# A two-layer hybrid decoder trunk: the mixer's products in joined 512-column form, its branches one after another, and its value products in pairs

## The chip, the core and the metric

The kernel runs on one core of one Trainium2 chip. A core has five engines with an instruction queue each: TensorE (PE; its weight loads are listed as PEld), VectorE (DVE), ScalarE (ACT), GpSimd (POOL) and SyncE (SP), which here issues the loads of weights. The metric is the device time of one execution in microseconds (us).

## The reference

Two layers of three residual blocks each on a sequence of 256 tokens of width 1024; all is float32.

```python
for l in range(DEPTH):
    x = x + 0.5 * swiglu(rmsnorm(x, norm_ffn1[l]), w_ffn1_in[l], w_ffn1_out[l])
    h = rmsnorm(x, norm_mix[l])
    x = x + hybrid_mixer(h, ...)
    x = x + 0.5 * swiglu(rmsnorm(x, norm_ffn2[l]), w_ffn2_in[l], w_ffn2_out[l])
# hybrid_mixer
a_qkv, b_q, b_kv, c_q, c_k, c_v, c_glow, c_r, gate_pre = jnp.split(h @ w_in, splits, axis=-1)
y_a = dilated_mixer(a_q, a_k, a_qkv[:, :, 2])          # 3 groups of 8 heads, merged by softmax denominators
o_b, _ = band_attention(...); y_b = o_b.reshape(...)   # 8 query heads on 2 key heads, with sinks
o_c = gla_chunked(...)                                 # gated linear attention, a recurrence over chunks
y_c = (rmsnorm(o_c, c_out_norm) * jax.nn.silu(c_r)).reshape(...)
gates = jax.nn.sigmoid(gate_pre.reshape(bn, s, N_BRANCH, D_MODEL))
merged = (gates[:, :, 0] * (y_a @ w_branch[0])
          + gates[:, :, 1] * (y_b @ w_branch[1])
          + gates[:, :, 2] * (y_c @ w_branch[2]))
return merged @ w_out
```

## The kernel before

Every matrix product is made in three parts, since TensorE takes the operands in a rounded float32 form. A weight w is split into hi, the rounded w, and lo = w - hi; the activation x likewise into two parts. The sum hi*x_hi + hi*x_lo + lo*x_hi stands for w*x. Weights come from memory as "raw" tiles of 128x1024 (four buffers); for each *unit* of 8 weight blocks of 128x128, ACT casts raw to hi (L191) and DVE subtracts to get lo (L192). There are five buffers each of hi and lo, and the split runs four units ahead of the product, so the split of unit u+5 can begin only when the product of unit u no longer needs its hi (ACT) and its lo (DVE).

A product with 256 tokens as columns has two forms:

- `mm3` (L330): three matmuls of 256 columns for each block, with three weight loads (L331, L332, L333), all into one 256-column half of a PSUM bank.
- `mmw` (L335): the two parts of x lie side by side in one tile, so that hi is loaded once for 512 columns (L341), and lo once for 256 columns (L343). The bank then holds two halves, which `joined` (L345) adds: ACT copies the upper half to a tile "low" (L347), DVE adds (L348).

Before the change the feed-forward blocks use `mmw`, and the mixer's feature-major products use `mm3`: the keys and queries of the linear attention (ck, cq), the 24 gate products, the three branch projections (12 units) and the output product w_out (8 units), 48 units in each layer. Token-major products (`tok_proj`, L541 to L543) are not touched.

PSUM has eight banks: four ("mm") rotate through these products, four ("at") through attention, transposes and the norm. A bank is free when the last reader of its former tile is done.

The attention ("att") and the linear recurrence ("gla") are generators; `fill` advances them by a rate after each product, so that their steps stand between the products on PE. After the gates all generators are run to the end, then the branches are taken per pair of output tiles (`mp`), all three branches in turn, and the merged tile is split once more into hi and lo (mh, ml), the input of w_out.

The program is written in this order, but a scheduler of the framework, which simulates it, decides at build time in which order each engine's instructions stand. Each engine then works through its list in that order and waits, where it must, with all that stands behind.

Other lines named below: the sum of squares of the norm is made on PE by L315, taken up by DVE in L316; POOL makes the reciprocal root r from it (L256), and PE spreads r over partitions (L324). L560 and L565 are the rotary embedding's products on DVE, which read a product's bank, L606 the scaling of the rotated key, L579 a transpose on PE, L571 and L597 small steps around POOL's root. L686 is the product of attention weights and values (AV), L761 a POOL copy that spreads a merge weight over a head.

## Time and profile before

| | before |
|---|---|
| median of 3 runs | 1452.05 us (1452.04 to 1452.5) |
| profiled execution, its own time | 1451.91 us |
| span of the trace | 1449.8 us |
| PE / PEld busy | 1439.2 us (99%) / 1268.1 us (87%) |
| DVE / ACT / POOL busy | 1053.7 us (73%) / 834.3 us (58%) / 137.9 us (10%) |
| data from memory | 246.31 MB, mean 170 GB/s |
| granted clock of PE | 0.999 of 2.4 GHz |

The span is what the trace covers; the execution's own time has 2.1 us more around it. The chain of waits goes back from the last instruction and tells which engine the time was spent on. A duration is that of one instruction's record. Records of instructions that follow each other on an engine overlap a little, so the pace of a series is read from starts, not from durations.

### The profile page before, as it was taken

The page shows a single profiled execution, that of the slowest core. Times are in us where ns is not written, and L with a number is a line of the kernel's source. Part 1 is how long each engine was busy: PE and PEld are TensorE (multiplying, and loading weights), DVE is VectorE, ACT ScalarE, POOL GpSimd, SP SyncE. Part 2 cuts the span into 40 slices and gives each one's busy share as a digit, 9 for nine tenths or more (in the row PEclk, how much of TensorE's full clock was granted, in tenths as well). Part 3 has the DMA queues.
Part 4 walks back from the last instruction along what each step waited for, and adds up shares of the span by engine and source line. Part 5 has one row for each costly group of instructions (what it writes and reads, how often), then busy time and mean ns, then how long its engine had stood idle before and what let it go on. Part 6 is the DMA issues. An engine that isn't in the chain of part 4 may idle for free.

```text
span 1449.8 us, 23394 instructions
## 1 busy us (share of the span) xinstructions
PE 1439.2 (99%) x9114; PEld 1268.1 (87%) x9114; DVE 1053.7 (73%) x1923; ACT 834.3 (58%) x1432; POOL 137.9 (10%) x124
## 2 busy tenths in 40 slices
PE   8999999999999999999999999999999999999998
PEld 6888898888899998888888888988878999988887
DVE  6887667888677687776677766688876767776753
ACT  6665456556747456565466555466477464566542
POOL 2030012223111000000000000131210200000000
PEclk9999999999999999999999999999999999999999
DMA  9665564443552565655665655643444426565651
GB/s 297 213 197 172 170 213 146 146 145 117 156 164 74 176 217 179 199 178 178 196 195 183 194 170 168 208 153 128 147 144 146 146 74 218 175 204 176 198 183 54
DMA packets 214702, 246.31 MB, mean 170 GB/s; under 512 B 6524, under 2 KB 183376, under 8 KB 214592
## 3 DMA queue, kind: packets, MB, share of 16 engines
q1 hardware_dynamic: 214016, 243.48, 52.2%
q0 software_dynamic: 544, 1.33, 0.4%
q8 instruction: 71, 1.16, 0.3%
q14 instruction: 39, 0.32, 0.1%
q10 hardware_dynamic: 32, 0.01, 0.0%
HBM read 243.76 MB, written 1.05 MB: 169 GB/s over the span
## 4 chain that ended last, share of the span: by engine, by line
PE 95%; DVE 2%; ACT 1%; POOL 1%; DMA 1%; issue 0%; SPq 0%; DVEq 0%
PE p L341 30%; PE p L343 16%; PE p L333 6%; PE p L331 6%; PE p L332 6%; PE p L541 6%; PE p L543 5%; PE p L542 5%; PE p L650 2%; PE p L686 2%; PE p L579 1%; PE p L485 1%; PE p L486 1%; PE p L487 1%; PE p L695 1%; PE p L874 1%
## 5 line engine op out<-in xcount | busy, mean ns | idle before, releaser
L191 ACT CAST hi<-raw 128x1024 fp32r<-128x1024 f32 (+3 forms) x468 | 484.2, 1037 | 509.1 <-PE p L341 270.9
L192 DVE TENSOR_TENSOR lo<-raw,hi 128x1024 fp32r<-128x1024 f32 (+3 forms) x468 | 564.8, 1209 | 255.1 <-ACT hi L191 249.2
L341 PE MATMUL p<-a,hi 128*128 128x512 f32 x1936 | 491.3, 394 | 1.5 <-ACT hi L191 1.2
L341 PEld LDWEIGHTS p<-a,hi 128*128 128x128 f32 x1936 | 348.5, 189 | 65.4 <-ACT hi L191 2.5
L343 PEld LDWEIGHTS p<-a,lo 128*128 128x128 f32 x1936 | 265.4, 190 | 19.3
L343 PE MATMUL p<-a,lo 128*128 128x256 f32 x1936 | 272.1, 282 | 0.0
L333 PE MATMUL p<-a,lo 128*128 128x256 f32 x768 | 219.0, 285 | 0.0
L331 PE MATMUL p<-a,hi 128*128 128x256 f32 x768 | 218.1, 285 | 0.0
L332 PE MATMUL p<-a,hi 128*128 128x256 f32 x768 | 218.0, 284 | 0.0
L256 POOL TENSOR_TENSOR s<-s,neghalf 128x8 f32<-128x8 f32 (+2 forms) x42 | 90.8, 2161 | 974.7 <-DVE s L316 656.1
L541 PE MATMUL p<-hi,a 128*128 128x512 f32 (+1 forms) x416 | 163.5, 393 | 0.0
L542 PE MATMUL p<-lo,a 128*128 128x512 f32 (+1 forms) x416 | 162.1, 390 | 0.0
L543 PE MATMUL p<-hi,a 128*128 128x512 f32 (+1 forms) x416 | 161.3, 389 | 0.0
L333 PEld LDWEIGHTS p<-a,lo 128*128 128x128 f32 x768 | 147.0, 191 | 1.4 <-issue 1.4
L332 PEld LDWEIGHTS p<-a,hi 128*128 128x128 f32 x768 | 147.0, 191 | 0.7 <-issue 0.3
L331 PEld LDWEIGHTS p<-a,hi 128*128 128x128 f32 x768 | 146.6, 191 | 1.1 <-issue 0.7
L541 PEld LDWEIGHTS p<-hi,a 128*128 128x128 f32 x416 | 79.3, 191 | 16.0 <-issue 0.7
L542 PEld LDWEIGHTS p<-lo,a 128*128 128x128 f32 x416 | 79.3, 191 | 14.6 <-issue 0.3
L543 PEld LDWEIGHTS p<-hi,a 128*128 128x128 f32 x416 | 79.0, 191 | 15.0 <-issue 0.3
L347 ACT COPY low<-p 128x256 f32<-128x256 f32 x200 | 74.5, 372 | 0.7 <-PE p L343 0.5
L348 DVE TENSOR_TENSOR w<-p,low 128x256 f32<-128x256 f32 x176 | 73.4, 418 | 0.0
L671 ACT ACTIVATE w<-w,st,s 128x128 f32<-128x128 f32 (+1 forms) x96 | 47.8, 504 | 11.7 <-DVE st L665 11.7
(224 smaller groups left out, 1294.7 us busy)
## 6 DMA issues: line engine op xcount, KB each, us to landing
raw<-in_w_ffn_in_dram SPq DMA_DIRECT2D x87, 1024.0 KB, 5.1
raw<-in_w_in_dram SPq DMA_DIRECT2D x76, 1024.0 KB, 5.1
raw<-in_w_ffn_out_dram SPq DMA_DIRECT2D x34, 1024.0 KB, 5.3
raw<-in_w_branch_dram SPq DMA_DIRECT2D x24, 512.0 KB, 3.4
raw<-in_w_ffn_out_dram SPq DMA_DIRECT2D x12, 768.0 KB, 4.5
raw<-in_w_out_dram SPq DMA_DIRECT2D x8, 1024.0 KB, 5.7
raw<-in_w_in_dram SPq DMA_DIRECT2D x4, 512.0 KB, 3.8
a<-in_x_dram SPq DMA_DIRECT2D x4, 256.0 KB, 4.6
```

The source lines that it names most:

```text
L191: nc.scalar.copy(hi[:, k:k + cut], r[:, k:k + cut])
L192: nc.vector.tensor_sub(lo[:, k:k + cut], r[:, k:k + cut], f(hi[:, k:k + cut]))
L256: nc.gpsimd.tensor_tensor(dst, src, neghalf[:, 0:n], op=OP.pow)
L331: nc.tensor.matmul(ps, wh, xh, start=first, stop=False)
L332: nc.tensor.matmul(ps, wh, xl, start=False, stop=False)
L333: nc.tensor.matmul(ps, wl, xh, start=False, stop=last)
L341: nc.tensor.matmul(ps, wh[:, k, :], xhl[k], start=first and k == 0, stop=False)
L343: nc.tensor.matmul(ps[:, 0:T], wl[:, k, :], xhl[k][:, 0:T], start=False, stop=last and k == nk - 1)
L347: nc.scalar.copy(low, ps[:, T:2 * T])
L541: nc.tensor.matmul(o, xh, wh[:, k - k0, :], start=(k == 0), stop=False)
L542: nc.tensor.matmul(o, xh, wl[:, k - k0, :], start=False, stop=False)
L543: nc.tensor.matmul(o, xl, wh[:, k - k0, :], start=False, stop=(k == KD - 1))
```

## The change

The mixer's products all use `mmw` with `joined`. Each 256-column product now takes a bank of its own (before, two shared one), and the gate's and key's scaling (L985, L990 before) reads the joined tile instead of the bank. The branches are taken in the order 2, 0, 1, each with all its four mp before the next; before a branch, only the generator that it needs is run to the end (`waits`), so that the other generators' steps may stand between its products; the weights of the branches are loaded in that order. Branch outputs are kept as tiles with both parts side by side (`y_parts`: twice as many instructions of half the size). The merged tile is split per 256 columns when the last branch has been added (L1056, L1057). w_out is taken in pairs of output tiles, the first pair in two steps of 6 and 2 blocks. In the attention, two AV groups are issued together. In the changed kernel the lines of the helpers are: split cast L192 and subtraction L193, `mmw` L337 and L339, `joined` L343 and L344, norm L316, L317 and L325, transpose L575.

```diff
+ORDER = (2, 0, 1)
...
-                for mp in range(KD // 2):
-                    for i in range(3):
+                for i in ORDER:
+                    for mp in range(KD // 2):
...
-
-    def mm3(ps, wh, wl, xh, xl, first, last):
-        nc.tensor.matmul(ps, wh, xh, start=first, stop=False)
-        nc.tensor.matmul(ps, wh, xl, start=False, stop=False)
-        nc.tensor.matmul(ps, wl, xh, start=False, stop=last)
...
-        def feat_proj(o):
-            wh, wl = chunk()
-            for k in range(KD):
-                mm3(o, wh[:, k, :], wl[:, k, :], n.h[k], n.l[k], k == 0, k == KD - 1)
+        def feat_proj():
+            ps = bank("mm")
+            mmw(ps, chunk(), n.hl, True, True)
+            return ps
...
-                    if pts:
-                        av(*pts.pop())
                     pts.append((i0, pt))
                     yield
-                av(*pts.pop())
+                    if len(pts) == 2:
+                        for a in pts:
+                            av(*a)
+                        pts.clear()
                 yield from done(t, o) if sink is None else done(t, o, nb, den)
 
         yT = [[None] * 4 for _ in range(3)]
+        merged = []
 
         def new_y(i):
             yT[i] = [big(F32R) for _ in range(4)]
 
         def y_parts(i, e, cols, src):
 
-            hv, lv = v3(yT[i][e], 2)[:, :, cols], v3(yT[i][2 + e], 2)[:, :, cols]
-            nc.scalar.copy(hv, src)
-            nc.vector.tensor_sub(lv, src, f(hv))
+            for u in range(2):
+                hv, lv = yT[i][2 * e + u][:, 0:T][:, cols], yT[i][2 * e + u][:, T:2 * T][:, cols]
+                nc.scalar.copy(hv, src[:, u])
+                nc.vector.tensor_sub(lv, src[:, u], f(hv))
...
+            merged.append(True)
...
-        ps = bank("mm")
-        feat_proj(ps[:, 0:T])
+        pk = [feat_proj()]
...
-        feat_proj(ps[:, T:2 * T])
+        pk.append(feat_proj())
         ck = big()
-        nc.vector.tensor_mul(v3(ck, 2), v3(ps, 2), rb2)
-        ps = bank("mm")
         for j in range(2):
-            feat_proj(ps[:, j * T:(j + 1) * T])
+            joined(ck[:, j * T:(j + 1) * T], pk[j])
+        nc.vector.tensor_mul(v3(ck, 2), v3(ck, 2), rb2)
         cq = big()
-        nc.vector.scalar_tensor_tensor(v3(cq, 2), v3(ps, 2), HD ** -0.5, rb2, op0=OP.mult, op1=OP.mult)
+        for j in range(2):
+            joined(cq[:, j * T:(j + 1) * T], feat_proj())
+        nc.vector.scalar_tensor_tensor(v3(cq, 2), v3(cq, 2), HD ** -0.5, rb2, op0=OP.mult, op1=OP.mult)
...
-            ps = bank("mm")
+            g = big()
             for j in range(2):
-                feat_proj(ps[:, j * T:(j + 1) * T])
+                ps = feat_proj()
                 fill()
-            g = big()
-            nc.vector.tensor_mul(v3(g, 2), v3(ps, 2), rb2)
+                joined(g[:, j * T:(j + 1) * T], ps)
+            nc.vector.tensor_mul(v3(g, 2), v3(g, 2), rb2)
             nc.scalar.activation(g, g, AF.Tanh, scale=0.5)
             gates.append(g)
-        while streams:
-            for name in list(streams):
-                step(name)
-        mh, ml = [], []
-        for mp in range(KD // 2):
-            acc = gates[mp]
-            for i in range(3):
-                wh, wl = chunk()
-                ps = bank("mm")
+        def waits(i):
+            return ("att" in streams and not merged) if i == 0 else ("att" if i == 1 else "gla") in streams
+
+        mhl = []
+        for i in ORDER:
+            while waits(i):
+                for name in list(streams):
+                    step(name)
+            for mp in range(KD // 2):
+                acc, g = gates[ORDER[0] * 4 + mp], gates[i * 4 + mp]
+                w = chunk()
+                o = wrk()
                 for j in range(2):
-                    for k in range(4):
-                        sl = slice((k % 2) * T, (k % 2) * T + T)
-                        mm3(ps[:, j * T:(j + 1) * T], wh[:, k, j * P:(j + 1) * P], wl[:, k, j * P:(j + 1) * P],
-                            yT[i][k // 2][:, sl], yT[i][2 + k // 2][:, sl], k == 0, k == 3)
-                g = gates[i * 4 + mp]
-                nc.vector.scalar_tensor_tensor(g, g, 1.0, ps, op0=OP.add, op1=OP.mult)
-                if i:
-                    nc.vector.tensor_add(acc, acc, g)
-            h, lo = big(F32R), big(F32R)
-            nc.scalar.copy(h, acc)
-            nc.vector.tensor_sub(lo, acc, f(h))
-            mh.append(h)
-            ml.append(lo)
-        for m in range(KD):
-            wh, wl = chunk()
-            ps = bank("mm")
-            for k in range(KD):
-                sl = slice((k % 2) * T, (k % 2) * T + T)
-                mm3(ps[:, 0:T], wh[:, k, :], wl[:, k, :], mh[k // 2][:, sl], ml[k // 2][:, sl], k == 0, k == KD - 1)
-            nc.vector.scalar_tensor_tensor(xT[m], ps[:, 0:T], 0.5, xT[m], op0=OP.mult, op1=OP.add)
-            nxt(m)
+                    ps = bank("mm")
+                    mmw(ps, [a[:, :, j * P:(j + 1) * P] for a in w], yT[i], True, True)
+                    joined(o[:, j * T:(j + 1) * T], ps)
+                    fill()
+                nc.vector.scalar_tensor_tensor(g, g, 1.0, o, op0=OP.add, op1=OP.mult)
+                if i == ORDER[0]:
+                    continue
+                nc.vector.tensor_add(acc, acc, g)
+                if i == ORDER[2]:
+                    for j in range(2):
+                        hl = big(F32R)
+                        a = acc[:, j * T:(j + 1) * T]
+                        nc.scalar.copy(hl[:, 0:T], a)
+                        nc.vector.tensor_sub(hl[:, T:2 * T], a, f(hl[:, 0:T]))
+                        mhl.append(hl)
+        for m0 in range(0, KD, 2):
+            ws = [chunk(), chunk()]
+            pss = [bank("mm"), bank("mm")]
+            for ks in (slice(0, KD - 2), slice(KD - 2, KD)) if m0 == 0 else (slice(0, KD),):
+                for j in range(2):
+                    mmw(pss[j], [w[:, ks, :] for w in ws[j]], mhl[ks], ks.start == 0, ks.stop == KD)
+            for j in range(2):
+                m = m0 + j
+                tmp = sm.tile([P, T], F32, tag="res", bufs=2, name=nm("res"))
+                joined(tmp, pss[j])
+                nc.vector.scalar_tensor_tensor(xT[m], tmp, 0.5, xT[m], op0=OP.mult, op1=OP.add)
+                nxt(m)
```

**Start of the mixer, DVE.** After the last step of the norm's sum (acc190), L316 (now L317) takes the sum from PE's bank p240; lo74 to lo76 are splits of weights for units 74 to 76. Before:

```order
L300 TENSOR_TENSOR acc190_1666<-acc190_1666,sq220_2101 128x256
L316 TENSOR_SCALAR s241_2202<-p240_2201 128x4
L192 TENSOR_TENSOR lo74_2214<-raw39_2002,hi74_2213 128x1024
L192 TENSOR_TENSOR lo75_2295<-raw39_2002,hi75_2294 128x1024
L972 SCALAR_TENSOR_TENSOR s229_2132<-s242_2208 128x4
L973 TENSOR_SCALAR s230_2133<-s242_2208 128x4
```

After:

```order
L301 TENSOR_TENSOR acc190_1666<-acc190_1666,sq220_2101 128x256
L193 TENSOR_TENSOR lo74_2214<-raw39_2002,hi74_2213 128x1024
L317 TENSOR_SCALAR s241_2202<-p240_2201 128x4
L193 TENSOR_TENSOR lo75_2288<-raw39_2002,hi75_2287 128x1024
L193 TENSOR_TENSOR lo76_2320<-raw40_2024,hi76_2319 128x1024
L971 SCALAR_TENSOR_TENSOR s229_2132<-s242_2208 128x4
```

The first reading of the norm's sum now stands behind the split lo74, and one more split (lo76) ahead of the small steps that use r.

**Start of the mixer, PE.** p240 is the norm's bank, s242 its root r. Between the sum's matmuls (L315, now L316) and this place stand 31 instructions of products before, and 15 after (14 of 256 columns, L339, and one of 512, L337). Before:

```order
L331 MATMUL p266_2324<-a188_1661,hi72_2145 128x256
L332 MATMUL p266_2324<-a188_1661,hi72_2145 128x256
L333 MATMUL p266_2324<-a188_1661,lo72_2146 128x256
L331 MATMUL p266_2324<-a195_1794,hi72_2145 128x256
L324 MATMUL p240_2201<-cst_70,s242_2208 128x128 x2
L332 MATMUL p266_2324<-a195_1794,hi72_2145 128x256
```

After:

```order
L339 MATMUL p265_2286<-a215_2086,lo71_2065 128x256
L339 MATMUL p265_2286<-a219_2098,lo71_2065 128x256
L325 MATMUL p240_2201<-cst_70,s242_2208 128x128 x2
L337 MATMUL p270_2316<-a184_1650,hi72_2145 128x512
L337 MATMUL p270_2316<-a188_1661,hi72_2145 128x512
```

What stands behind r's spreading is now the first product into bank p270, the bank of the token product p238, which L556 and L561 (L560 and L565 before) still have to read; before, p266 had been begun ahead of it, and no bank of p238 or p239 was needed for ck and cq.

**Start of w_out, DVE.** lo161 and lo162 are splits for the fourth and fifth unit of w_out; p779 and p781 are the two halves of the last branch unit; a683, a693 are merged tiles and a762 the first of the eight split tiles for w_out. Before:

```order
L192 TENSOR_TENSOR lo161_5634<-raw88_5431,hi161_5633 128x1024
L1046 SCALAR_TENSOR_TENSOR a674_5261<-a674_5261,p692_5637 128x512
L1048 TENSOR_TENSOR a611_4560<-a611_4560,a674_5261 128x512
L192 TENSOR_TENSOR lo162_5671<-raw89_5468,hi162_5670 128x1024
L1051 TENSOR_TENSOR a694_5665<-a611_4560,a693_5664 128x512
L1060 SCALAR_TENSOR_TENSOR xT0_106<-p695_5674,xT0_106 128x256
```

After:

```order
L193 TENSOR_TENSOR lo161_5534<-raw88_5319,hi161_5533 128x1024
L344 TENSOR_TENSOR w771_5500<-p774_5513,low775_5522 128x256
L1051 TENSOR_TENSOR a683_4873<-a683_4873,a630_4517 128x512
L1048 SCALAR_TENSOR_TENSOR a648_4634<-a648_4634,w764_5461 128x512
L344 TENSOR_TENSOR w778_5537<-p779_5538,low780_5547 128x256
L1048 SCALAR_TENSOR_TENSOR a659_4716<-a659_4716,w771_5500 128x512
L193 TENSOR_TENSOR lo162_5573<-raw89_5352,hi162_5572 128x1024
L344 TENSOR_TENSOR w778_5537<-p781_5550,low782_5559 128x256
L1057 TENSOR_TENSOR a762_5451<-a683_4873,a762_5451 128x256
L1051 TENSOR_TENSOR a693_4941<-a693_4941,a648_4634 128x512
```

The join of the last half (L344 of p781) and the first part for w_out (L1057, a762) now stand behind lo162; the four merged tiles come ready one after another behind it.

**Start of w_out, PE.** hi157 and lo157 are the last branch unit's weights, hi158 to hi161 those of w_out. Before:

```order
L332 MATMUL p692_5637<-a571_4301,hi157_5502 128x256
L333 MATMUL p692_5637<-a569_4299,lo157_5503 128x256
L331 MATMUL p695_5674<-a678_5362,hi158_5535 128x256
L332 MATMUL p695_5674<-a679_5363,hi158_5535 128x256
L333 MATMUL p695_5674<-a678_5362,lo158_5536 128x256
```

After:

```order
L339 MATMUL p781_5550<-a680_4858,lo157_5388 128x256
L339 MATMUL p781_5550<-a681_4859,lo157_5388 128x256
L337 MATMUL p785_5580<-a762_5451,hi158_5420 128x512
L337 MATMUL p786_5581<-a762_5451,hi159_5457 128x512
L337 MATMUL p796_5646<-a762_5451,hi160_5496 128x512
L337 MATMUL p797_5647<-a762_5451,hi161_5533 128x512
L337 MATMUL p785_5580<-a763_5454,hi158_5420 128x512
```

Before, the first product of w_out takes a678 and a679, made from the first merged tile, which was complete nine units earlier; now it takes a762, and four products take each tile in turn.

## Rows read from the trace of the kernel before

**Rows 1.** Busy time and share of the span of each engine, and the chain of waits by engine.

```profile
PE 1439.2 (99%) x9114; PEld 1268.1 (87%) x9114; DVE 1053.7 (73%) x1923; ACT 834.3 (58%) x1432; POOL 137.9 (10%) x124
PE 95%; DVE 2%; ACT 1%; POOL 1%; DMA 1%; issue 0%; SPq 0%; DVEq 0%
```

**Rows 2.** What PE waited for between 25 and 1440 us, all of it: total us, times, longest.

```profile
PE p L579 <- DVE a L599: 0.6, 2, 0.3
```

**Rows 3.** The chain in a feed-forward stretch (`mmw`): start us, length us, what.

```profile
601.59 1.84 PE p L341 x8
603.43 0.95 PE p L343 x8
...
612.76 1.84 PE p L341 x8
```

**Rows 4.** The chain in the branch stage (`mm3`), the first and the last of 34 pieces without a gap: start us, length us, what.

```profile
517.98 0.12 PE p L332
...
521.94 0.12 PE p L332
```

**Rows 5.** Groups of instructions by line and shape: busy us, mean ns of one.

```profile
L331 PE MATMUL p<-a,hi 128*128 128x256 f32 x768 | 218.1, 285 | 0.0
L192 DVE TENSOR_TENSOR lo<-raw,hi 128x1024 fp32r<-128x1024 f32 x436 | 534.1, 1227 | 242.0 <-ACT hi L191 240.3
L348 DVE TENSOR_TENSOR w<-p,low 128x256 f32<-128x256 f32 x176 | 73.4, 418 | 0.0
L191 ACT CAST hi<-raw 128x1024 fp32r<-128x1024 f32 x436 | 457.3, 1052 | 476.9 <-PE p L341 240.9 <-PE p L332 90.1 <-PE p L543 71.3
L347 ACT COPY low<-p 128x256 f32<-128x256 f32 x200 | 74.5, 372 | 0.7 <-PE p L343 0.5 <-ACT hi L191 0.2
```

**Rows 6.** The timeline of PE around one AV group: start us, us, engine, line.

```profile
457.91 0.28 PE L331 MATMUL p<-a,hi 128*128 128x256 f32 x1
458.03 0.28 PE L332 MATMUL p<-a,hi 128*128 128x256 f32 x1
458.24 0.66 PE L686 MATMUL p<-w,a 128*64 128x128 f32 x8
458.83 0.39 PE L333 MATMUL p<-a,lo 128*128 128x256 f32 x1
459.05 0.28 PE L331 MATMUL p<-a,hi 128*128 128x256 f32 x1
```

**Rows 7.** Busy us of each engine by stretch: the branches, w_out, feed-forward products (columns: stretch, its length, PE, PEld, DVE, ACT, POOL, clock, DMA share, GB/s).

```profile
495.00:520.00 25.00, 25.00 (x211) 25.00 (x210) 21.45 (x27) 11.35 (x12) 0.00 (x0) 1.00 0.81 256
520.00:545.00 25.00, 25.00 (x210) 24.96 (x209) 20.27 (x34) 14.15 (x24) 0.00 (x0) 1.00 0.53 171
560.00:700.00 140.00, 140.00 (x803) 123.19 (x802) 100.72 (x146) 81.94 (x133) 0.00 (x0) 1.00 0.57 186
```

**Rows 8.** The start of the mixer on PE: the last token product that uses hi69 (L543) in the timeline, then L315 and L324 in the chain.

```profile
208.28 0.42 PE L543 MATMUL p<-hi,a 128*128 128x272 f32 x2
...
208.82 0.81 PE p L315 x8
209.63 0.23 PE p L333
...
213.45 0.45 PE p L324 x4
```

**Rows 9.** The same place on DVE, timeline; the brackets give the idle time before and what ended it.

```profile
209.67 0.16 DVE L316 TENSOR_SCALAR s<-p 128x4 f32<-128x4 f32 x1 [3.59 <-PE p L315]
...
211.00 1.22 DVE L192 TENSOR_TENSOR lo<-raw,hi 128x1024 fp32r<-128x1024 f32 x1
212.14 0.15 DVE L972 SCALAR_TENSOR_TENSOR s<-s 128x4 f32<-128x4 f32 x1
...
213.39 0.35 DVE L565 TENSOR_TENSOR w<-p,S 128x64 f32<-128x64 f32 x2
...
216.43 0.48 DVE L606 TENSOR_TENSOR a<-a,s 128x128 f32<-128x128 f32 x2
...
217.04 0.35 DVE L565 TENSOR_TENSOR w<-p,S 128x64 f32<-128x64 f32 x2
...
220.49 0.49 DVE L606 TENSOR_TENSOR a<-a,s 128x128 f32<-128x128 f32 x2
```

**Rows 10.** The same place on POOL and ACT, timeline.

```profile
208.78 2.00 ACT L191 CAST hi<-raw 128x1024 fp32r<-128x1024 f32 x2 [3.98 <-issue]
...
209.91 2.08 POOL L256 TENSOR_TENSOR s<-s,neghalf 128x4 f32<-128x4 f32 x1 [107.73 <-DVE s L316]
...
217.26 0.72 POOL L429 TENSOR_TENSOR C<-cosT,hn 128x64 f32<-128x64 f32 x2 [1.20 <-DVE a L560]
217.95 1.58 POOL L430 TENSOR_TENSOR S<-sinT,hn 128x64 f32<-128x64 f32 x2
219.50 0.69 POOL L256 TENSOR_TENSOR s<-s,neghalf 128x2 f32<-128x2 f32 x1
```

**Rows 11.** The end of the branches and the start of w_out on DVE and ACT, timeline.

```profile
521.78 1.05 ACT L191 CAST hi<-raw 128x1024 fp32r<-128x1024 f32 x1 [1.82 <-PE p L332]
...
521.86 0.69 DVE L1046 SCALAR_TENSOR_TENSOR a<-a,p 128x512 f32<-128x512 f32 x1 [0.33 <-PE p L333]
522.58 0.69 DVE L1048 TENSOR_TENSOR a<-a,a 128x512 f32<-128x512 f32 x1
523.19 1.22 DVE L192 TENSOR_TENSOR lo<-raw,hi 128x1024 fp32r<-128x1024 f32 x1
524.33 0.69 DVE L1051 TENSOR_TENSOR a<-a,a 128x512 fp32r<-128x512 f32 x1
528.46 0.42 DVE L1060 SCALAR_TENSOR_TENSOR xT<-p,xT 128x256 f32<-128x256 f32 x1 [3.44 <-PE p L333]
```

**Rows 12.** The merge of the attention groups: POOL's spreading copies, and PE's transposes of them, timeline.

```profile
417.31 1.21 POOL L761 COPY w<-cd 128x512 f32<-128x512 f32 x2 [11.02 <-DVE cd L787]
418.48 4.26 POOL L761 COPY w<-ce 128x512 f32<-128x512 f32 x4
...
422.11 0.60 PE L579 MATMUL p<-cst,w 128*128 128x128 f32 x4
423.99 0.60 PE L579 MATMUL p<-cst,w 128*128 128x128 f32 x4
```

## The prediction, made before the changed kernel ran

> **What bounds the kernel now.** I read the busy shares and the chain of waits first: PE is busy 99% of the span and carries 95% of the chain, DVE 2% [rows 1]. The reader is to see that no other engine sets the end. Then PE's waits: between 25 and 1440 us it waited 0.6 us in all [rows 2]. So two things decide: how long PE's own instructions take, each 0.12 us less being 0.12 us less of time, and whether the new order makes PE wait where it did not, each such wait being added in full. Third come the stretches: in the branches DVE is busy 21.45 of 25 us, in w_out 20.27 of 25, in the feed-forward 100.72 of 140 [rows 7]; DVE is the next engine and has least room where the change adds work to it. Last the timelines of three places where PE goes from one kind of product to another.
>
> **What PE saves.** A unit of eight blocks takes (612.76 - 601.59)/4 = 2.792 us as `mmw` [rows 3], 0.349 us a block. As `mm3` the pieces follow each other every (521.94 - 517.98)/33 = 0.120 us [rows 4], 0.360 us a block. 768 blocks change form [rows 5]: 768 x 0.011 = 8.4 us. Whether a block's halves come four or eight in a row changes nothing that rows 3 show (8 x 0.230 + 8 x 0.119), so the branches get the same price.
>
> The Trainium skill, "TensorE: Matmul & The Clock Gate", section "Back-to-back issue gap", gives 262 cycles at 2.4 GHz for 256 columns and 518 for 512. By that the pace would be 0.327 us a block before and 0.325 after, an estimate of 1.9 us saved instead of 8.4. Rows 3 and 4 have both forms on this kernel, slower than the page's and further apart, and they decide; what the 6.5 us between would make is the fourth rival.
>
> The AV products: changing from a full-array product to AV and back costs 0.21 - 0.12 = 0.09 us going in (458.03 to 458.24) and 0.22 - 0.12 = 0.10 coming out [rows 6]. Of 40 groups 8 fall together with others, and by the order there are 14 changes fewer: 14 x 0.095 = 1.3 us. Other changes between products and small matmuls also get fewer, and no row prices each of them; from 1.3 up to twice what rows 6 have, 2.7; I take 2. Sum: 8.4 + 2 = 10.4 us saved, 9.7 to 11.1.
>
> **What the other engines get.** 120 joins in all, each 0.372 us on ACT and 0.418 on DVE [rows 5]: 45 and 50 us on engines with 615 and 396 us idle in the span. Starts on DVE come about 0.08 before the record's end (lo at 523.19 lasts 1.22, the next starts at 524.33 [rows 11]): I count 1.14 for a split, 0.61 for 512 columns, 0.33 for 256. Per branch unit DVE then has 1.14 + 2 x 0.33 + 0.61 = 2.41 us in the first branch, 3.02 in the second (one addition more), 3.68 in the third (two split parts more), against 2.79 on PE. PE's idle-free pace hides the first; in the third DVE falls behind, and this shows at its end, priced below. The gates' scaling from a joined tile costs what it did from the bank within 0.02 us, and `y_parts` in twice as many pieces some 0.1 us each; both lie beside products, and cost that little only if uncovered. The branch weights are the same bytes in another order, at a DMA share of 0.81 before [rows 7]; four raw buffers remain: nothing.
>
> **The waits that the order adds**, worked out by following each list on the durations of before.
>
> *Start of w_out.* Before, w_out's first product needed a merged tile that was nine units old. Now all four merged tiles are completed in the last branch, and DVE's list has the split lo162 ahead of the last join, and the first tile for w_out (L1057, a762) behind both. Let T be the end of the last branch product. hi157 is needed until its four wide matmuls are through, 4 x 0.12 = 0.48 before T, so the cast of hi162 starts 0.4 before T and ends at T + 0.65 (1.05, rows 11); lo162 ends at T + 1.8, the join at T + 2.1, L1057 at T + 2.55, PE goes on at T + 2.6. That is the lower end. But between lo161 and lo162 stand five instructions, 0.33 + 0.61 + 0.61 + 0.33 + 0.61 = 2.5 us; lo161 itself can start only a unit earlier by the same rule, T - 2.79 + 0.65 = T - 2.1, and ends at T - 1.0, so lo162 starts at T + 1.5 instead of 0.65: the wait is 3.45. Then PE uses up each tile in 4 x 0.23 = 0.92 us, and DVE needs 0.61 + 0.61 + 0.33 = 1.55 before a769: 0.6 more. 4.05 a layer, 2.6 to 4.6. Both layers' lists are alike here.
>
> *Start of the mixer.* Before, L316 took the sum when PE had made it, POOL's root started at 209.91 and took 2.08, and PE came to r only at 213.45, 3.8 us after the sum [rows 8 to 10]. Now PE has 14 x 0.12 + 0.23 = 1.9 us of products there, and DVE's list has lo74 ahead of L317. With the last use of hi69 at 208.70: the cast follows at 208.78, lo74 from 209.86 to 211.0 [rows 9, 10]. PE's sum is done 0.47 + 0.81 after 208.70, at 210.0; L317 runs at 211.0, the root from 211.24 to 213.32; PE is there at 211.9 and waits 1.5. Without lo74 it would be 0.5. Next, unit 72's bank is p238's, which the rotary steps still read: L565 ends 213.74 - 211.99 = 1.75 after r [rows 9, 10], so at 215.1, with PE at 213.85 after the spreading's 0.45: 1.2. Then the transpose of the first key tile, L606 ending 4.9 after r, at 218.2 against 217.9: 0.35; the second bank (L565 of the second, 5.4 after r): 0.3; and the second key tile, where POOL makes the next layer's tables from 217.26 to 219.50 ahead of the second root [rows 10] and L606 ends 9.0 after r [rows 9]: 222.3 against 221.5, 0.8. Sum 4.2 in the first layer (1.5 + 1.2 + 0.35 + 0.3 + 0.8); the second has no such tables and its last term goes: 3.4. Bounds 2 (if the bank waits fall away because ACT and DVE get there earlier) and 5.
>
> *Merge.* Six spreads of four transposes stood some 2 us apart; now they stand together, 6 x 0.44 = 2.6 us on PE, while POOL needs 422.74 - 417.31 = 5.4 us for the copies [rows 12]. Before, PE came 4.8 us after POOL began. How early it comes now depends on more steps than rows show: 0 if as late, 5.4 - 2.2 = 3.2 if at once; I take 0.8, near the late end, since the copies are still let go by the same chain.
>
> **Sum**, against the profiled execution's 1451.9: -10.4 + 2 x 4.05 + 4.2 + 3.4 + 2 x 0.8 = +6.9, so 1458.8. The median of the runs is 0.1 above that execution, which changes nothing here. With the lower ends of all waits (2 x 2.6 + 2 x 2 = 9.2) and the larger saving it is -1.9, 1450.0; with the upper ends and the smaller saving, 2 x 4.6 + 2 x 5 + 2 x 3.2 - 9.7 = +15.9, 1468.
>
> **Rivals.**
> *The waits at their lower ends.* The rotary steps free their banks before PE asks, and DVE has no backlog at lo162. For: DVE idles 3.59 us before L316 in the trace of before, so it is not always behind [rows 9]. Against: the casts set these starts, and they follow PE's own releases. 1450, between no change and faster.
> *The order hides all of it.* Both lists are made by the same scheduler, and in before it left PE 0.6 us of waits [rows 2]; it may have put lo162 and lo74 ahead because they are early on the chip as well. Then the saving stands alone: 1441.5. Against: the release of hi157 and hi69 cannot come before PE's last use, whatever the list. This is the other side.
> *DVE becomes the bound of the last two branches.* 4 x 3.02 + 4 x 3.68 = 26.8 us of work against 8 x 2.79 = 22.3: if the splits may not wait, 4.5 us a layer pile up, and steps of attention placed between the products come on top at one or two us. The wait at w_out is then 6 instead of 4: 1463. For: 21.45 of 25 busy already [rows 7]. Against: the extra operations stand behind the splits in the list, which PE needs first.
> *The joined products save less.* If the new 4-block halves only reach the smaller saving of 1.9, the sum is 1465. Against: rows 3.
>
> **Chances.** Forecast 0.43, lower ends 0.22, all hidden 0.15, DVE bound 0.15, less saved 0.05. A measurement of this kernel tells no less than about 0.2%, 2.9 us, from no change. The forecast's own range is 1455 to 1462. Slower by over 0.2%: the forecast but for its edge, 0.39, + 0.15 + 0.05 = 0.59. The lower ends split into 0.12 same and 0.10 faster: same 0.04 + 0.12 = 0.16, faster 0.15 + 0.10 = 0.25. The range 1445 to 1465 leaves out most of the all-hidden case and little above.
>
> **What would show it.** The changed profile should have L337 at 8 in 1.84 us and L339 at 8 in 0.95 also in the mixer; PE waits of about 3.5 us behind L1057 and 1.5 ahead of L325 (on POOL or DVE), twice each; PE's busy time down by some 10 us while its idle time is up by some 17. If PE's waits sum to less than 10 us, the forecast is wrong in its waits; if the busy time falls by less than 8, in its saving.

## The result and the profile after

| | before | after |
|---|---|---|
| median of the runs | 1452.05 us | 1466.27 us (1465.24 to 1467.71, 5 runs) |
| profiled execution | 1451.9 us | 1467.71 us (span 1465.9) |
| ratio, with its 95% interval | | 1.0099 [1.0088, 1.0110] |

The change made the kernel 14.2 us slower. The direction was forecast; the time lies 7.5 us above the forecast and 1.3 us above the range.

The busy shares and the chain of the kernel after, to be held against [rows 1]:

```profile
PE 1438.3 (98%) x8346; PEld 1231.0 (84%) x8346; DVE 1087.3 (74%) x2071; ACT 870.0 (59%) x1580; POOL 135.1 (9%) x124
...
PE 92%; DVE 3%; ACT 2%; POOL 1%; DMA 1%; issue 0%; SPq 0%; DVEq 0%; ACTq 0%
```

PE has 768 instructions fewer and is as long busy as before. PE's share of the chain fell from 95% to 92%; DVE and ACT have 1% more each. What PE waited for between 25 and 1460 us (total us, times, longest), to be held against the 0.6 us of [rows 2]:

```profile
PE p L337 <- DVE a L1057: 7.0, 2, 3.5
PE p L537 <- DVE w L561: 3.7, 2, 1.9
PE p L325 <- POOL s L257: 2.5, 2, 1.3
PE p L337 <- DVE w L561: 2.2, 2, 1.1
PE p L575 <- DVE a L713: 1.4, 2, 0.7
PE p L575 <- DVE a L595: 0.6, 2, 0.3
```

17.4 us, so 16.8 more. The first line is w_out's first product, the third and fourth are the start of the mixer, the fifth is the merge, the last was there before. The second, token products that wait for their bank, stands in no step of the forecast.

The other thing that had not been forecast is in the windows (columns: stretch, length, busy us of PE, PEld, DVE, ACT, POOL, granted clock, DMA share, GB/s):

```profile
215.00:217.00 2.00, 1.28 (x3) 1.12 (x4) 1.17 (x7) 0.43 (x2) 0.70 (x1) 0.64 1.03 398
217.00:219.00 2.00, 2.00 (x6) 1.51 (x6) 1.61 (x9) 0.00 (x0) 0.92 (x3) 0.51 0.11 40
219.00:221.00 2.00, 2.00 (x15) 1.83 (x14) 0.92 (x4) 1.60 (x3) 1.37 (x4) 1.00 0.02 4
...
530.00:532.00 2.00, 2.00 (x6) 1.57 (x5) 2.00 (x6) 0.71 (x2) 0.00 (x0) 0.50 0.00 0
```

Behind PE's waits its granted clock is 0.50 for some microseconds, and wide matmuls (512 columns) start 0.43 us apart, eight of them between 215.72 and 219.14; at 1.00 they start 0.23 apart [rows 3]. At w_out the first five still start 0.23 to 0.38 apart, and the slow ones follow. Both layers have this at both places; no other 25 us window of the mixers is below 1.00. The Trainium skill, "TensorE: Matmul & The Clock Gate", section "What's actually happening", names two states of the clock, 1.2 and 2.4 GHz, and says that activity releases the lower one. The 0.50 and 1.00 here agree; 0.51 and 0.64 are windows with both.

The start of the first mixer (timeline of PE, DVE and POOL: start us, us, engine, line; in brackets the wait ahead), where [rows 8 to 10] were read before:

```profile
213.88 0.71 PE L325 MATMUL p<-cst,s 128*128 128x128 f32 x4 [1.28 <-POOL s L257]
215.72 3.58 PE L337 MATMUL p<-a,hi 128*128 128x512 f32 x8 [1.12 <-DVE w L561]
...
210.49 1.22 DVE L193 TENSOR_TENSOR lo<-raw,hi 128x1024 fp32r<-128x1024 f32 x1 [4.29 <-ACT hi L192]
211.63 0.15 DVE L317 TENSOR_SCALAR s<-p 128x4 f32<-128x4 f32 x1
215.22 0.35 DVE L561 TENSOR_TENSOR w<-p,S 128x64 f32<-128x64 f32 x2
...
211.86 1.96 POOL L257 TENSOR_TENSOR s<-s,neghalf 128x4 f32<-128x4 f32 x1 [109.49 <-DVE s L317]
```

The split lo74 runs ahead of L317 although DVE had idled for 4.29 us before it: the list holds the sum back until the split is through. Root and spreading follow it, and then the rotary steps free the bank at 215.6 (215.22 + 0.35). The end of the branches, where [rows 11] were read:

```profile
528.76 6.63 PE L337 MATMUL p<-a,hi 128*128 128x512 f32 x21 [3.48 <-DVE a L1057]
...
523.12 1.23 DVE L193 TENSOR_TENSOR lo<-raw,hi 128x1024 fp32r<-128x1024 f32 x1 [0.31 <-ACT hi L192]
524.26 0.42 DVE L344 TENSOR_TENSOR w<-p,low 128x256 f32<-128x256 f32 x1
524.60 0.68 DVE L1051 TENSOR_TENSOR a<-a,a 128x512 f32<-128x512 f32 x1
525.20 0.68 DVE L1048 SCALAR_TENSOR_TENSOR a<-a,w 128x512 f32<-128x512 f32 x1
525.80 0.41 DVE L344 TENSOR_TENSOR w<-p,low 128x256 f32<-128x256 f32 x1
526.13 0.68 DVE L1048 SCALAR_TENSOR_TENSOR a<-a,w 128x512 f32<-128x512 f32 x1
526.73 1.22 DVE L193 TENSOR_TENSOR lo<-raw,hi 128x1024 fp32r<-128x1024 f32 x1
527.87 0.41 DVE L344 TENSOR_TENSOR w<-p,low 128x256 f32<-128x256 f32 x1
528.20 0.41 DVE L1057 TENSOR_TENSOR a<-a,a 128x256 fp32r<-128x256 f32 x1
```

DVE works without a gap from 523.12 on, and PE's first tile is the last of these lines. Where the loss came up, by the starts of the stages' first matmuls on PE, after less before, in layer 1: up to the first gate product (start of the mixer and token products) +5.5, gates -1.2, branches -0.7, w_out with its wait +4.4; layer 2 the same within 0.1. Together 16.1 us, as the spans have it (1465.9 - 1449.8); the executions' own times lie 15.8 apart.

### The profile page after: what moved, and what is told of

It is laid out like the page before. It is cut to its first block, busy times and chain, and to the rows that moved or that the text cites. A ratio compares the mean times of both kernels' runs of the same rounds, so it can differ in the third digit from the quotient of the medians.

```text
span 1465.9 us, 22244 instructions
## 1 busy us (share of the span) xinstructions
PE 1438.3 (98%) x8346; PEld 1231.0 (84%) x8346; DVE 1087.3 (74%) x2071; ACT 870.0 (59%) x1580; POOL 135.1 (9%) x124
## 4 chain that ended last, share of the span: by engine, by line
PE 92%; DVE 3%; ACT 2%; POOL 1%; DMA 1%; issue 0%; SPq 0%; DVEq 0%; ACTq 0%
PE p L337 43%; PE p L339 22%; PE p L537 5%; PE p L539 5%; PE p L538 5%; PE p L682 2%; PE p L646 1%; PE p L481 1%; PE p L483 1%; PE p L482 1%; PE p L575 1%; DVE lo L193 1%; PE p L691 1%; POOL s L257 1%; PE p L874 1%; ACT hi L192 1%
## 5 line engine op out<-in xcount | busy, mean ns | idle before, releaser
L193 DVE TENSOR_TENSOR lo<-raw,hi 128x1024 fp32r<-128x1024 f32 (+3 forms) x468 | 564.6, 1208 | 276.8 <-ACT hi L192 270.9
L192 ACT CAST hi<-raw 128x1024 fp32r<-128x1024 f32 (+3 forms) x468 | 483.6, 1036 | 447.1 <-PE p L337 328.8
L337 PE MATMUL p<-a,hi 128*128 128x512 f32 x2704 | 700.7, 398 | 10.7 <-DVE a L1057 7.0
L337 PEld LDWEIGHTS p<-a,hi 128*128 128x128 f32 x2704 | 488.0, 191 | 100.5 <-issue 8.3
L339 PEld LDWEIGHTS p<-a,lo 128*128 128x128 f32 x2704 | 374.5, 190 | 29.6 <-issue 0.3
L339 PE MATMUL p<-a,lo 128*128 128x256 f32 x2704 | 386.3, 282 | 0.0
L343 ACT COPY low<-p 128x256 f32<-128x256 f32 x320 | 119.0, 372 | 25.2 <-PE p L339 13.7
L344 DVE TENSOR_TENSOR w<-p,low 128x256 f32<-128x256 f32 x224 | 91.8, 416 | 0.3 <-ACT low L343 0.3
L538 PEld LDWEIGHTS p<-lo,a 128*128 128x128 f32 x416 | 79.4, 191 | 14.2
L654 DVE CUSTOM_DVE_ANT_0 w<-p,cst 128x128 f32<-128x128 f32 (+1 forms) x128 | 33.2, 317 | 7.8 <-PE p L646 7.8
L481 PE MATMUL p<-hi,a 128*128 128x512 f32 x88 | 34.2, 389 | 0.0
L482 PE MATMUL p<-lo,a 128*128 128x512 f32 x88 | 34.2, 389 | 0.0
L483 PE MATMUL p<-hi,a 128*128 128x512 f32 x88 | 34.2, 389 | 0.0
L467 DVE TENSOR_TENSOR a<-w,a 128x256 fp32r<-128x256 f32 x88 | 33.1, 417 | 0.0
L462 DVE TENSOR_TENSOR w<-w,w 128x512 f32<-128x512 f32 x44 | 30.6, 697 | 2.3 <-ACT w L461 1.0
```

The costliest lines, as they stand in the source:

```text
L192: nc.scalar.copy(hi[:, k:k + cut], r[:, k:k + cut])
L193: nc.vector.tensor_sub(lo[:, k:k + cut], r[:, k:k + cut], f(hi[:, k:k + cut]))
L337: nc.tensor.matmul(ps, wh[:, k, :], xhl[k], start=first and k == 0, stop=False)
L339: nc.tensor.matmul(ps[:, 0:T], wl[:, k, :], xhl[k][:, 0:T], start=False, stop=last and k == nk - 1)
L343: nc.scalar.copy(low, ps[:, T:2 * T])
L344: nc.vector.tensor_add(dst, ps[:, 0:T], low)
```

## Experiments

The theory after the result: three new waits (mixer start, token products, w_out), each a matter of what stands ahead of the releaser in DVE's or ACT's list, and PE at half clock behind some of them. The rivals: joined products are not cheaper at all in the mixer; or DVE has become the bound there; or a wait goes only to come back elsewhere. Every ratio is to the kernel before in runs on the same chip (medians 1451.7 to 1452.2); differences between numbers, and to after, can be across chips.

**1. The products ck and cq as before, `mm3` into the halves of a bank.**

```diff
-        pk = [feat_proj()]
+        ps = bank("mm")
+        feat_half(ps[:, 0:T])
...
-        for j in range(2):
-            joined(cq[:, j * T:(j + 1) * T], feat_proj())
+        for j in range(2):
+            feat_half(ps[:, j * T:(j + 1) * T])
```

> The changed kernel with the four key and query products of the linear attention made as before: three 256-column matmuls a block, two products to a bank, no joins. If the start of the mixer is lost to the banks of the token product and to the shorter cover of the norm's root, PE's waits there (1.3 and 1.1 us in each layer) go, the clock stays at 1.00 there, and the time falls by about 2 x 4.4 us less 2 x 0.35 us of products that are longer again: 1458. If the split lo74 ahead of the norm's sum is the cause by itself, a wait of about 1 us stays ahead of the spreading and the time is 1462 or above.

1461.44 us (1460.32 to 1462.77), ratio 1.0066 [1.0051, 1.0081]: 4.8 less than after, and 3.4 above the 1458 expected. No wait is left at the mixer start, and the clock stays at 1.00 there. But DVE's list is another one as well (its timeline):

```profile
209.83 0.16 DVE L317 TENSOR_SCALAR s<-p 128x4 f32<-128x4 f32 x1 [3.60 <-PE p L316]
210.02 2.36 DVE L193 TENSOR_TENSOR lo<-raw,hi 128x1024 fp32r<-128x1024 f32 x2
```

The sum stands ahead of the splits here, as before the change, so this run does not tell what lo74's place costs by itself. It would have been covered: with `mm3` PE comes to the spreading of r only at 213.45, 1.3 us behind the root's end (210.08 + 2.08), and the place of lo74 costs about 1.0 (L317 runs 2.0 us behind the start of PE's sum in after, 1.0 before).

**2. The value products one group at a time.**

```diff
-                    if len(pts) == 2:
-                        for a in pts:
-                            av(*a)
-                        pts.clear()
+                    if pts:
+                        av(*pts.pop())
+                    pts.append((i0, pt))
+                    yield
+                av(*pts.pop())
```

> The changed kernel with the attention's value products issued one group at a time, as before. If pairing the groups moved the exponentials ahead of the rotary steps' square on ACT, the wait of 1.9 us for the bank in the middle of the token products goes in both layers: 3.8 us less, given back in part by up to 2 us of changes between products, 1463 to 1465. If that wait comes from the 4 us by which all is later, or from the scheduler's list whatever the groups, it stays and the time is 1466 to 1468.

Four runs: 1461.62, 1463.18, 1467.28 and 1468.25 us, at granted clocks of 1.000, 0.997, 0.994 and 0.993; ratio 1.0099 [1.0081, 1.0117]. The median, 1465.23, is not clear of after's. The 1.9 us wait of the token products is gone. How it came about is in the timelines of after and of this kernel. After:

```profile
352.69 1.03 ACT L192 CAST hi<-raw 128x1024 fp32r<-128x1024 f32 x1
353.63 0.58 ACT L554 ACTIVATE w<-p 128x512 f32<-128x512 f32 x1
...
354.90 0.68 DVE L556 TENSOR_TENSOR a<-p,C 128x512 f32<-128x512 f32 x1
355.50 0.74 DVE L561 TENSOR_TENSOR w<-p,S 128x256 f32<-128x256 f32 x2
356.39 0.47 PE L537 MATMUL p<-hi,a 128*128 128x512 f32 x1 [1.87 <-DVE w L561]
```

Value products one at a time:

```profile
350.29 0.58 ACT L554 ACTIVATE w<-p 128x512 f32<-128x512 f32 x1
350.76 1.04 ACT L192 CAST hi<-raw 128x1024 fp32r<-128x1024 f32 x1
...
351.50 0.75 DVE L561 TENSOR_TENSOR w<-p,S 128x256 f32<-128x256 f32 x2
...
352.76 1.22 DVE L193 TENSOR_TENSOR lo<-raw,hi 128x1024 fp32r<-128x1024 f32 x1
```

With pairs, the cast of a weight chunk stands ahead of the rotary steps' square on ACT (L554), and its split ahead of their products on DVE, which free the bank; without, both stand behind, as they did before the change. It is the cast and the split that moved ahead, not the exponentials that were expected. The second finding is the spread of the four runs, which goes with the clock. The profiled execution is the 1461.62 one, and it has no half clock behind waits of the same lengths as after's:

```profile
215.97 2.10 PE L337 MATMUL p<-a,hi 128*128 128x512 f32 x8 [1.13 <-DVE w L561]
526.86 2.09 PE L337 MATMUL p<-a,hi 128*128 128x512 f32 x8 [3.48 <-DVE a L1056]
529.25 3.26 PE L337 MATMUL p<-a,hi 128*128 128x512 f32 x13 [0.29 <-DVE a L1056]
```

That prices the clock. At the mixer start eight wide matmuls take 2.10 here and 3.58 after, 1.5 us. At w_out 21 take 529.25 + 3.26 - 526.86 = 5.65 and after 6.63, 1.0 us. Layer 2 gives the same within 0.1: 5.0 us in all. The pairs make the value products 1.6 us shorter on PE (23.9 us before and here, 22.3 after, from each one's start to the next start) and bring 3.7 us of waits.

**3. The halving of the merged tile on GpSimd.**

```diff
-                        nc.vector.tensor_sub(hl[:, T:2 * T], a, f(hl[:, 0:T]))
+                        nc.gpsimd.tensor_sub(hl[:, T:2 * T], a, f(hl[:, 0:T]))
```

> The changed kernel with the second part of the merged tile (the subtraction ahead of w_out) on GpSimd instead of VectorE, so that the first tiles for w_out do not stand behind the split lo162 in VectorE's list. If that place in the list makes the wait, the 3.5 us go, and with them the half clock behind it (1.65 us): 2 x 5.1 us less, 1456; the last tile of the merge then still needs the last join, up to 1 us each. If the wait is a chain of dependences from the last branch product, it stays at 2.6 us or more and the time is above 1463.

1469.27 us (1467.06 to 1470.92), ratio 1.0119 [1.0104, 1.0134]: no gain. Timeline around w_out:

```profile
523.96 0.71 ACT L1056 CAST a<-a 128x256 fp32r<-128x256 f32 x2
...
524.45 2.52 POOL L1057 TENSOR_TENSOR a<-a,a 128x256 fp32r<-128x256 f32 x2 [59.82 <-ACT a L1056]
...
524.63 1.74 DVE L193 TENSOR_TENSOR lo<-raw,hi 128x1024 fp32r<-128x1024 f32 x1
525.35 0.96 PE L337 MATMUL p<-a,hi 128*128 128x512 f32 x3 [2.17 <-POOL a L1057]
```

A subtraction takes POOL 1.26 us, DVE 0.41; the cast of the tile stands behind other work on ACT; and DVE's split takes 1.74 instead of 1.22 while POOL subtracts. The Trainium skill, "GPSIMD Engine Reference", section "Specifications", lists SBUF interfaces shared with VectorE, with contention for VectorE's instructions of two SBUF inputs; the split's 1.74 agrees. The releaser moved, the wait only shrank and split up (4 times, 5.7 us in all), and a new wait of 2.6 us for the joins' `res` came behind. The time is that of the expectation's second case, but POOL's own pace makes the wait here, so the run does not tell whether the place in DVE's list alone made the 3.5 us.

**4. Fourteen unread matmuls ahead of w_out, to keep PE busy in the wait.** Their result is read by nobody; the chunks of w_out are taken in the same order.

```diff
+        pre = [chunk() for _ in range(4)]
+        keep = bank("at")
+        for _ in range(14):
+            nc.tensor.matmul(keep, pre[3][1][:, 0, :], yT[ORDER[2]][1], start=True, stop=True)
         for m0 in range(0, KD, 2):
-            ws = [chunk(), chunk()]
+            ws = [pre.pop(0) if pre else chunk() for _ in range(2)]
```

> The changed kernel with 14 added matmuls of 512 columns between the last branch product and w_out, whose result nobody reads: they fill the 3.5 us in which PE waits there. All other lists are the same. If the matmuls after the wait are slow because the clock was lowered while PE idled, the granted clock stays at 1.00 through the start of w_out, 21 wide matmuls take about 4.8 us instead of 6.5, and the time falls by 2 x 1.0 to 2 x 1.7 us: 1463 to 1464.5. If they are slow because each takes another bank or because VectorE uses the same memory, nothing changes: 1466 to 1467.

1465.12 us (1464.62 to 1467.11), ratio 1.0094 [1.0079, 1.0109].

```profile
523.89 3.36 PE L1062 MATMUL p<-a,lo 128*128 128x512 f32 x14
527.53 2.09 PE L337 MATMUL p<-a,hi 128*128 128x512 f32 x8 [0.28 <-DVE a L1057]
529.92 3.25 PE L337 MATMUL p<-a,hi 128*128 128x512 f32 x13 [0.30 <-DVE a L1057]
```

The clock stays at 1.00 through w_out in both layers, and the 21 matmuls take 5.64 us instead of 6.63, with the 0.30 of wait for the third tile within it. Only 0.45 us a layer of that 1.0 is left at the end: at the next norm PE then loses 0.5 us around a wait of 0.2, which the half clock had hidden. The median is 0.6 above the range expected. The mean clock of the four runs, 0.998 to 0.999, lies above after's 0.995 to 0.997. So idling, not the joined form, makes the clock fall here, and what the clock costs is partly given back by the waits behind it. At the start of the mixer, which this edit leaves alone, the eight wide matmuls took 2.08 us in layer 1 and 3.24 in layer 2 behind waits of the same lengths: the fall does not come each time.

**5. Before, with joined gate products alone.**

```diff
-            for j in range(2):
-                feat_proj(ps[:, j * T:(j + 1) * T])
-                fill()
+            for j in range(2):
+                ps = feat_joined()
+                fill()
+                joined(g[:, j * T:(j + 1) * T], ps)
...
```

> The kernel before with only the 24 gate products of a layer joined; key, query, branch and output products, their order and the attention as before. If the joined form saves 0.087 us a unit wherever it is and only the places around it cost, 48 units save 4.2 us and no new wait comes: 1447.5, PE's waits stay at 0.6 us and the clock at 1.00. If the joins themselves load VectorE and ScalarE so that PE waits, the time is 1450 or above.

1452.52 us (1451.75 to 1452.71, 10 runs), ratio 1.0002 [0.9993, 1.0011]: nothing gained. PE's waits:

```profile
PE p L584 <- DVE a L770: 1.6, 2, 0.8
PE p L341 <- DVE a L348: 1.1, 1, 1.1
```

(The 0.6 us that was there before is left out.) Reckoned on PE from each matmul's start to the next one's, with waits taken out, the feature products take 4.9 us less in both layers (48 units by 0.088 are 4.2), and the small matmuls between them 2.5 us more; the seam between two kinds counts to the one ahead of it. Against the 2.5 us that remain stand 2.7 us of new waits, at the merge (two of 0.8) and for a join that frees its bank late (1.1). That the joined form is not cheaper falls: its products are, and what they save goes into waits for other engines and into the small matmuls. Why those cost more was not tried.

**6. Number 5 with joined w_out. 7. Number 6 with joined branches, in the old branch order.** In both the old order of branches, and no unfinished steps between.

```diff
-                mm3(ps[:, 0:T], wh[:, k, :], wl[:, k, :], mh[k // 2][:, sl], ml[k // 2][:, sl], k == 0, k == KD - 1)
...
+                mmw(ps, [a[:, ks, :] for a in w], mhl[ks], ks.start == 0, ks.stop == KD)
...
-                        mm3(ps[:, j * T:(j + 1) * T], wh[:, k, j * P:(j + 1) * P], wl[:, k, j * P:(j + 1) * P],
-                            yT[i][k // 2][:, sl], yT[i][2 + k // 2][:, sl], k == 0, k == 3)
+                    mmw(ps, [a[:, :, j * P:(j + 1) * P] for a in w], yT[i], True, True)
+                    joined(o[:, j * T:(j + 1) * T], ps)
```

> As the run before, with the output product w_out joined too, its input split per 256 columns, in the old order of the branches (all three per pair of tiles). Its first products take six tiles that are complete long before, so if the wait at w_out comes from the order of the branches and not from the joined form, none comes here: 0.09 us for each of 16 units less, 1446. If the split ahead of the tiles makes the wait, PE waits here as well, 1 us or more a layer and 1449 or above.

> As the run before, with the branch products joined too, still all three branches per pair of tiles. VectorE then has about 1.14 + 0.67 + 0.61 + 0.41 + 0.17 = 3.0 us a unit against PE's 2.8 over 12 units. If VectorE's load in the branches is what makes PE wait at w_out, a wait of 1 to 3 us a layer comes back, with half clock behind it at times: 1447 to 1452. If only the order of the branches makes it, 0.07 us for each of 24 units are saved: 1444.5.

1454.14 us, ratio 1.0015 [1.0006, 1.0024], and 1453.4 us, 1.0009 [1.0000, 1.0018]; both expected to fall well below before if the order alone made w_out's wait; neither did. PE's waits in number 7:

```profile
PE p L341 <- DVE res L348: 2.6, 2, 1.3
PE p L341 <- DVE w L348: 1.9, 2, 1.0
```

These are waits for banks: a joined bank comes free only after copy and addition. In neither is there a wait for merged tiles. So w_out's 3.5 us come from the new branch order, in which all tiles are finished in the last branch, and not from the joined form by itself.

**8. After, with the last branch in `mm3` without joins.**

```diff
+                if i == ORDER[2]:
+                    o = bank("mm")
+                    for j in range(2):
+                        for k in range(4):
+                            y = yT[i][k]
+                            mm3(o[:, j * T:(j + 1) * T], w[0][:, k, j * P:(j + 1) * P], w[1][:, k, j * P:(j + 1) * P],
+                                y[:, 0:T], y[:, T:2 * T], k == 0, k == 3)
...
```

> The changed kernel with the last of the three branches made in three 256-column matmuls a block, two products to a bank, without joins: VectorE has 0.67 us less for each of the last four units, and its list has the first two tiles for w_out ahead of the split lo162. If VectorE's load in the last branch makes the wait of 3.5 us, it falls below 1 us and the half clock behind it goes: 2 x 3 to 2 x 5 us less, 1456 to 1460. If the chain from the last product's release through the split decides, the wait stays above 2.5 us and the time at 1465 to 1467.

1460.18 us (1459.77 to 1461.91), ratio 1.0060 [1.0043, 1.0076], at the upper edge of what was expected. PE goes from the branch into w_out without a wait; the first stands ahead of the fifth tile, 0.5 us, with a bank wait of 1.0 behind (from the waits, then PE's timeline):

```profile
PE p L342 <- DVE res L349: 2.1, 2, 1.0
...
524.14 3.82 PE L342 MATMUL p<-a,hi 128*128 128x512 f32 x16
528.43 1.43 PE L342 MATMUL p<-a,hi 128*128 128x512 f32 x5 [0.47 <-DVE a L1071]
```

So the order puts the tiles last, and without the joins of that branch the wait is gone. The edit took 0.67 us of joins a unit from DVE, but its list changed too: the first two tiles (L1071) run at 520.98, ahead of the last two splits (522.85 and 526.22). Which of the two counts for how much is not separated.

**9. After, of which only the joined gates and the new order with its unfinished steps are kept**: ck, cq, branches and w_out in `mm3`, value products one at a time (the edits of 1, 2 and 8, for all branches, and for w_out `mm3` with `mhl[k][:, 0:T]` and `mhl[k][:, T:2 * T]`). **10. The same with joined w_out. 11. Number 9 with value products in pairs.**

> The changed kernel with only its gate products joined, and with its order of the branches and unfinished steps between them; key, query, branch and output products in three 256-column matmuls as before, value products singly. If the gates' saving was lost because the attention's steps had to be finished ahead of the branches, it is kept here: 4.2 us less than before and 1.4 us of wait in the merge, 1449. If it was lost to the waits of the steps themselves, the time is about that of the run with gates only, 1452.5. No wait above 0.6 us at w_out, since VectorE has no joins in the branches.

> As the run before, with the output product joined in pairs, as the change has it. If the joined form is worth 0.09 us a unit there, 1.4 us less than the run before. If its banks, which are free only after the copy on ScalarE and the addition on VectorE, make PE wait as in the run with gates and output joined (1.0 us a layer), 0.7 us more.

> As the first run of this set, with the value products in pairs, as the change has it. If pairing always brings the wait of 1.9 us for the bank in the middle of the token products, and saves 2.7 us of PE's own time, it is 1 us slower than the first; the wait should be in PE's list of waits twice.

| | median us (10 runs) | ratio to before |
|---|---|---|
| 9 | 1450.8 (1450.61 to 1451.09) | 0.9992 [0.9982, 1.0002] |
| 10 | 1452.15 (1451.8 to 1453.86) | 1.0001 [0.9991, 1.0010] |
| 11 | 1453.52 (1452.04 to 1456.09) | 1.0012 [1.0002, 1.0021] |

Number 9 is the fastest of all and lies between its two expected times, but its interval still holds 1. PE's new waits in it:

```profile
PE p L585 <- DVE a L722: 1.5, 2, 0.7
```

The 0.6 us that was there before comes on top. Number 10 adds the bank wait `res` (2.6 us) and is 1.35 slower than 9. Number 11 has the token products' wait again (3.7 us), so the pairs cause it under this order too; its runs at clock 1.0 take 1452.04 to 1452.93 us, those at 0.997 and 0.998 1454.5 to 1456.09.

The loss can now be laid out in steps from kernel to kernel, by medians from three chips and after's own: before to 9, -1.3; to 11, pairs, +2.7; to 1, joined branches and w_out, +7.9; to after, joined ck and cq, +4.8. Sum 14.1.

**12. Number 4 with ten more unread matmuls at the mixer start.**

```diff
         pk.append(feat_proj())
+        cw = [chunk()]
+        keep = bank("at")
+        for _ in range(10):
+            nc.tensor.matmul(keep, cw[0][1][:, 0, :], n.hl[KD - 1], start=True, stop=True)
...
```

> The changed kernel with unused matmuls in the waits at the start of the mixer too (10 of 512 columns, besides the 14 ahead of w_out). If the half clock behind the waits is what the time lies above the sum of waits and savings, and what makes the runs differ by some us, the granted clock is 1.00 throughout, the runs lie within 1 us of each other, and the time is 1460 to 1462. If the runs differ for another reason, they still do, and the time stays at 1464 to 1466.

1466.15 us (1464.8 to 1466.3), ratio 1.0094 [1.0078, 1.0110]: a miss (1460 to 1462 was expected). The clock stays at 1.00 at both starts of the mixer and of w_out; from the norm's sum to the first token product it is 1.1 and 1.5 us less than after. But the clock fell elsewhere, behind the 1.9 us wait of layer 2's token products:

```profile
1075.00:1100.00 25.00, 23.40 (x131) 18.18 (x132) 18.71 (x41) 18.26 (x38) 6.07 (x3) 0.93 0.40 127
```

Layer 2's token products take 1.5 us longer than in after and in number 4. After has the same wait without a fall there. Which of several waits of 1 to 4 us is followed by half clock differs between kernels and between executions of one kernel; what decides it stays open.

## Why the forecast was right in direction and short in size

- *PE is the bound and each new wait counts in full.* Right: there are 16.8 us of waits more, and the loss stands where they are. That this is close to the forecast's 17.3 is in part luck: 13.1 of it stands where the forecast had it, 3.7 at a place that it did not look at. By its own sign the forecast is wrong in its saving: PE's busy time fell by 0.9 us, not by some 10, and 5.0 of the difference are the clock.
- *w_out.* Right in mechanism and, for the first wait, in size: 3.45 worked out, 3.48 measured, behind lo162, five instructions and L1057 as listed. The further 0.6, ahead of the second merged tile, came as 0.3 at full clock (numbers 2 and 4) and not at all at half clock, since PE was slower than the tiles came.
- *Mixer start.* The wait for r was 1.28 against 1.5, the bank 1.12 against 1.2. The next terms (0.35, 0.3, 0.8) came as no wait, neither at half clock nor at full clock (number 2): these three were priced too high. POOL's root for the first key tile took 1.72 us before, where a split of DVE ran beside it (214.35 and 214.29), and 0.70 after, where none did (216.18); in number 2 the tile is ready at 217.98, 0.9 ahead of its transpose. So 2.4 us a layer of waits instead of 4.2 and 3.4.
- *Merge.* 0.71 against 0.8.
- *The term that was missing: the clock after a wait.* 5.0 us, from executions with waits of the same lengths with and without it. The step that failed first is the sum's pricing of a wait by its own length alone. The products behind w_out's and the mixer's waits took 1.0 and 1.5 us more a layer; the 1.0 is what is left after the small waits that half clock swallowed.
- *The wait that was not foreseen: the token products' bank.* 1.9 us a layer, 3.7 in all. The step "the AV products: 14 changes fewer" looked at PE's list only. The value products did get 1.6 us shorter (1.3 was worked out for them), but taking away the single groups let the cast and the split stand ahead of the rotary steps on ACT and DVE, which the forecast did not follow there.
- *"8.4 + 2 = 10.4 us saved".* The second step that failed: from 16.8 of waits, 5.0 of clock and 15.8 of loss, 6.0 us net are left, 4.4 less than forecast. The pace of the pieces is as priced (a branch unit 2.81 us instead of 2.88, a gate unit 0.09 less). Reckoned as in number 5, the feature products of number 2, whose profile has no half clock, take 7.5 us less than before, against 8.4; but the small matmuls of that kernel take 4.2 us more, most of it transposes (3.0). The forecast had the other changes between products and small matmuls as a saving of 0.7 (2 less 1.3), without a row for it. Why the transposes cost more stays open.
- *Rivals.* "Hides all" and "lower ends" fell with the waits. "DVE becomes the bound of the last branches" is half true: DVE has no gap ahead of w_out's first tile, and without the joins the wait goes (number 8, with its list changed too), but the wait is the 3.5 us of the forecast, not 6. "Joined products save less" is right as to the sum, for another reason than it gave: not the pace of the halves, but what stands between the products.

Added up: 10.4 of forecast saving less 6.0 makes +4.4; the clock +5.0; the unforeseen wait +3.7; waits that came smaller -2.9 (mixer), -1.1 (w_out) and -0.2 (merge). That is +8.9, by which the profiled execution lies above the forecast. The sum has to close, since the 6.0 is what was left over.

## What to carry to other kernels

When an order changes on the engine that bounds the kernel, follow the lists of its helpers at every place where a buffer is freed, also at those places that the edit does not name: a cast and a split ahead of the releaser cost 3.7 us here, more than the instructions saved. Price a wait of the bounding engine as its length plus what slower products behind it cost, and give this second part a range, since it comes in some executions and not in others. A cheaper form of product gained nothing here where its results must pass through two more instructions before their bank or tile is free. Where PE has banks and tiles to spare, it may pay: joined gates with the new order were 1.3 us faster than before, which is not clear of no change.

## What was unexpected of the hardware

- After waits of 1 to 3.5 us PE's granted clock was 0.50 for some microseconds, in some executions and not in others of one kernel: 1461.62 us at a mean of 1.000, 1468.25 at 0.993 (number 2). In one execution it fell in one layer and not in the other (number 4).
- The clock's loss can move: where fourteen or ten extra matmuls filled two waits, it fell behind a third, which it had left alone (number 12).
- A 128x1024 subtraction on DVE took 1.74 us instead of 1.22 while POOL subtracted (number 3). POOL's 128x2 root took 1.72 us beside such a subtraction (before) and 0.70 without (after).
